# Retention gates between the attention's pairs, decays added to the mask by an accumulating DMA

## The chip, the cores and the metric

The kernel runs on one core of one Trainium2 chip. The metric is the device time of one execution in microseconds (us): the median of three runs was 2032.78 us (2031.46 to 2033.83). A profile was taken of one further execution.

## What is computed

Two transformer blocks for 512 tokens of width 1024, in fp32. The change lies in the second block, which is two layers of this form:

```python
proj = x @ w_in
fq, fk, fv, f_logit, rq, rk, rv, rg = split(proj)
log_f = log_sigmoid(f_logit + b_forget)             # 8 heads
fox_out = fox_attention(fq, fk, fv, log_f)          # softmax(q k / 8 + c_i - c_j), causal, c = cumsum(log_f)
ret = retention(rotary(rq), rotary(rk) / sqrt(128), rv, gamma)   # 4 heads, decays gamma
ret_out = silu(rg) * head_groupnorm(ret)            # rg: the retention gate
x = layernorm(alpha * x + concat(fox_out, ret_out) @ w_out)
x = layernorm(alpha * x + square(relu(x @ w_ff1)) @ w_ff2)
```

The forgetting attention ("fox") has 8 heads of 64, which the kernel works off as four pairs; the retention has 4 heads of 128. The gate `rg` of retention head i is 128 of 512 columns of the projection.

## The kernel before, in words

Every fp32 operand of a matmul is split into a high and a low part (`split2`, line 329: ACT writes the high part, DVE the low one), and a product is three matmuls of 128x512. A weight block is 512 KB: SP loads `wr` (three buffers), ACT makes `wh`, DVE makes `wl` (six buffers each; `wblk`, line 350). `proj_a` (line 414) multiplies one block of 128 columns with all tokens, 24 matmuls into one PSUM bank; `proj_b` (line 419) takes four banks at once, one for each group of 128 tokens, and works through the weights in steps of 24 matmuls.

PSUM has eight banks: four with the tag "mm" for the projections (`mm_ps`, line 301) and four with the tag "at" for the attention and retention (`at_ps`, line 304). A bank is free for the next tile when the last reader of the old one is done.

The order of TensorE's work is written out by a planner, `Weave` (line 160). The main thread issues projections (priority 2); attention pairs and retention heads are threads of priority 1 that cut in when their due time, by the planner's own costs, is reached. A thread yields an event or a number of "at" banks that it needs. TensorE then executes exactly this order. The other engines (ACT, DVE, POOL, and SP, which issues most DMAs) each run their own queue in order; their order is set when the kernel is built, from the order of the code and what is ready.

In a layer of the second block (`block2`, line 1261) the main thread goes through: the values of the attention (line 1263); the forget logits, their cumulative sum, and a DMA that writes it to DRAM as `cd` (line 1270); four times q and k of a pair, after which the pair's thread is spawned (line 1285); the values of the retention (line 1287); four times q and k of a retention head with their rotation, after which its thread is spawned (line 1303); the four gates (line 1304); the output projection (line 1317), whose steps wait for the `mix` tiles they read: 0 to 3 from the attention's pairs, 4 to 7 from the retention heads.

An attention pair (line 507) first splits q and k of each of its two heads out of their PSUM banks (`qs`, `kh`, `kl`), and asks `bias` (line 1194) for the decays: `row` (called `cb` in the code) is a row of `cd` broadcast to 128 partitions by a DMA, and `cm` is that row plus a causal mask `tri`, added by POOL. Scores of a token group then go through DVE (one reduction with `row`, one with `cm` on the diagonal block), ACT (exp), DVE (1/sum) and back to TensorE for transposes and the product with the values.

A retention head (`ret_head`, line 1206) takes the rotated q and k (`ra`: two ACT copies, a DVE and two POOL operations), makes `inner` and the states, normalises on DVE and POOL (`ro`), waits for its gate `sg`, is transposed, multiplied by the gate (`rz`) and split into `mix`. `sg` itself is silu of the gate's projection: three ACT passes and one DVE product (lines 1305 to 1308).

All of these tiles, except weights and small ones, come out of one pool of 56 buffers of 128x512 (`bt`, line 290).

Of the kernel before, what the change touches and what calls it, by code (L numbers as in the profile page):

```python
# [11 lines left out]
F32R = mybir.dt.float32r  # L12
I32 = mybir.dt.int32
AF = mybir.ActivationFunctionType
ALU = mybir.AluOpType
# [4 lines left out]
P, T, D = 128, 512, 1024  # L20
# [13 lines left out]
def _blocks():  # L34

    out = []

    def a(name, l, c0, n, k=D, w=P):
        out.extend((name, l, 0, k, c, c + w, "") for c in range(c0, c0 + n, w))

    def b(name, l, k0, k1, c0):
        out.extend((name, l, k, k + 2 * P, c0, c0 + 512, "") for k in range(k0, k1, 2 * P))

    def low(name, l, c0, n):
        out.append((name, l, 0, D, c0, c0 + n, "low"))

    for c in (0, 512, 1024):
        b("w_in", 0, 0, D, c)
    low("w_in", 0, 3584, 16)
    a("w_in", 0, 1536, 1024)  # L50
    b("w_in", 0, 0, D, 2560)
    b("w_in", 0, 0, D, 3072)
    b("w_in", 0, 0, D, 3600)
    b("w_in", 0, 0, D, 4112)
    for i in range(4):
        for j in range(2):
            a("w_in", 0, 4624 + (2 * i + j) * P, P)
            a("w_in", 0, 5648 + (2 * i + j) * P, P)
        a("w_branch_moba", 0, 256 * i, 256, 512, 256)
        a("w_branch_gla", 0, 256 * i, 256)  # L60
    for n in range(2):
        b("w_out", 0, 0, D, 512 * n)

    def ffn(up, down, l):
        for h in range(2):
            a(up, l, 2048 * h, 2048)
            for n in range(2):
                b(down, l, 2048 * h, 2048 * (h + 1), 512 * n)

    ffn("w_up", "w_down", 0)  # L70
    for l in range(2):
        a("w_in_2", l, 0, 1024)
        low("w_in_2", l, 1536, 8)
        b("w_in_2", l, 0, D, 1024)
        a("w_in_2", l, 1544, 1024)
        b("w_in_2", l, 0, D, 2568)
        a("w_in_2", l, 3080, 512)
        for n in range(2):
            b("w_out_2", l, 0, D, 512 * n)
        ffn("w_ff1_2", "w_ff2_2", l)  # L80
    return out
# [186 lines left out]
def model_kernel(ctx: ExitStack, tc: tile.TileContext, I, out):  # L268
    nc = tc.nc
# [12 lines left out]
    wv = Weave(8 - NM)  # L282
    act, dve, pool = Engine(nc.scalar, wv, 0.2, 0.83), Engine(nc.vector, wv, 0.17, 1.04), Engine(nc.gpsimd, wv, 0.25, 2.1)
    uid = [0]

    def nm(s):
        uid[0] += 1
        return f"{s}_{uid[0]}"

    def bt(s="b", dt=F32):  # L290
        return pb.tile([P, T], dt, tag="b", name=nm(s))

    def at(s="a", dt=F32):
        return pa.tile([P, 4, T], dt, tag="a", name=nm(s))
# [28 lines left out]
    def copy(o, i):  # L323
        act.activation(o, i, AF.Copy)

    def sub_lo(o, x, hi, eng=dve):
        eng.tensor_tensor(o, x, hi.bitcast(F32), ALU.subtract)

    def split2(hi, lo, x, scale=None):

        if scale is None:
            copy(hi, x)
            sub_lo(lo, x, hi)
        else:
            act.activation(hi, x, AF.Copy if isinstance(scale, float) else AF.Identity, scale=scale)
            dve.scalar_tensor_tensor(lo, x, scale, hi.bitcast(F32), ALU.mult, ALU.subtract)
# [35 lines left out]
    class Acts:  # L372


        def __init__(self, n, s, groups=False):
            self.ev = [Event() for _ in range(max(n, NT))]
            if groups:
                self.h = [at(s + "h", F32R) for _ in range(n // 4)]
                self.l = [at(s + "l", F32R) for _ in range(n // 4)]
                self.hs = [self.h[k // 4][:, k % 4, :] for k in range(n)]  # L380
                self.ls = [self.l[k // 4][:, k % 4, :] for k in range(n)]
            else:
                self.hs = [bt(s + "h", F32R) for _ in range(n)]
                self.ls = [bt(s + "l", F32R) for _ in range(n)]

        def split(self, k, x, scale=None):

            split2(self.hs[k], self.ls[k], x, scale)
            wv.mark(self.ev[k])

# [23 lines left out]
    def proj_a(name, l, c, acts, k=8):  # L414
        ps = mm_ps()
        yield from form_a(ps, wblk(name, l, 0, k * P, c, c + P), 0, acts, range(k))
        return ps
# [29 lines left out]
    def const(n):  # L447
        src = const_src(n)
        t = bt(n)[:, 0 : src.shape[1]]
        load(t, src)  # L450
        return t
# [35 lines left out]
    def sigmoid(s, x):  # L487

        act.activation(s, x, AF.Exp, scale=-1.0)
        act.activation(s, s, AF.Ln, bias=one)  # L490
        act.activation(s, s, AF.Exp, scale=-1.0)
# [8 lines left out]
    def row_bcast(src, n0):  # L500

        t = bt("row")
        load(t, bass.AP(tensor=src.tensor, offset=src.offset + n0, ap=[[0, P], [1, T]]))
        return t
# [342 lines left out]
    xw = Acts(8, "xT", True)  # L847
# [342 lines left out]
        yield from block2(0, xw2, h)  # L1190


    def fox_bias(cd, tri):
        def bias(h):
            cb, cm = row_bcast(cd, T * h), bt("cm")
            pool.tensor_tensor(cm, cb, tri, ALU.add)

            def pieces(t):
                d = (P * t, P * t + P, cm[:, P * t : P * t + P])
                return [d] if t == 0 else [(0, P * t, cb[:, 0 : P * t]), d]  # L1200

            return pieces

        return bias
# [56 lines left out]
    def block2(l, xw, h):  # L1261
        fv = []
        yield from proj_b("w_in_2", l, 0, D, 1024, xw, to_tokens(fv, False), tail=8, wait_t=True)
        f = yield from low_proj(wblk("w_in_2", l, 0, D, 1536, 1544, "low"), 8, xw)
        a = bt("fa")
        dve.tensor_scalar(f[0:8], f[0:8], col(f"bf{l}")[0:8], None, ALU.add)
        log_sigmoid(f[0:8], f[0:8], a[0:8])
        dve.tensor_tensor_scan(a[0:8], one[0:8].to_broadcast([8, T]), f[0:8], 0.0, ALU.mult, ALU.add)
        cd = pd.tile([8, T], F32, tag="cd", name=nm("cd"))
        nc.sync.dma_start(cd, a[0:8])  # L1270
        bias = fox_bias(cd, const("tri"))
        mix = Acts(8, "mix")
        for i in range(4):
            qk = []
            for j in range(2):
                qk.append((yield from proj_a("w_in_2", l, 512 * j + P * i, xw)))

            def operands(q, k):
                def get():
                    return q, k, -0.125, None  # L1280
                    yield

                return get

            wv.spawn(attention_pair(i, operands(*qk), fv, bias, mix), 1)
        vs = []
        yield from proj_b("w_in_2", l, 0, D, 2568, xw, to_tokens(vs, False))
        ccos, csin = const("cc"), const("ss")
        decay, xi, zeta = const("decay"), const("xi"), const("zeta")
        sgs = []  # L1290
        for i in range(4):
            qk = []
            for j in range(2):
                ps = yield from proj_a("w_in_2", l, 1544 + 512 * j + P * i, xw)
                a, b = bt("ra"), bt("rb")
                copy(b[0:64], ps[64:128])
                copy(b[64:128], ps[0:64])
                dve.tensor_tensor(a, ps, ccos, ALU.mult)
                pool.tensor_tensor(b, b, csin, ALU.mult)
                pool.tensor_tensor(a, a, b, ALU.add)  # L1300
                qk.append(a)
            sgs.append([Event(), bt("sg")])
            wv.spawn(ret_head(l, i, *qk, vs, decay, xi, zeta, sgs[i], mix), 1)
        for i in range(4):
            ps = yield from proj_a("w_in_2", l, 3080 + P * i, xw)
            ev, sg = sgs[i]
            sigmoid(sg, ps)
            dve.tensor_tensor(sg, ps, sg, ALU.mult)
            wv.mark(ev)
        hT = Acts(8, "hT", True)  # L1310
        ln1 = LayerNorm(h, norm_rows("ln1_g_2", "ln1_b_2", l))

        def norm1(t):
            ln1.apply(t)
            yield from to_features(h[t], hT, t)

        yield from out_proj("w_out_2", l, mix, h, ALPHA, ln1.part, norm1)
        ln2 = LayerNorm(h, norm_rows("ln2_g_2", "ln2_b_2", l))
        if l == 0:
            xw2 = Acts(8, "xT", True)  # L1320

        def norm2(t):
            ln2.apply(t)
            if l == 0:
                yield from to_features(h[t], xw2, t)
            else:
                for n in range(2):
                    nc.sync.dma_start(token_rows(out, t, n), h[t][n])

        yield from ffn("w_ff1_2", "w_ff2_2", l, hT, h, ALPHA, ln2.part, norm2)  # L1330
        if l == 0:
            yield from block2(1, xw2, h)
# [45 lines left out]
```

## Time and profile before

| | |
|---|---|
| median of 3 runs | 2032.78 us |
| profiled execution | 2036.39 us |
| its span | 2034.3 us |
| PE (TensorE matmul) busy | 1992.4 us, 98% |
| DVE busy | 1149.8 us, 57% |
| ACT busy | 954.1 us, 47% |
| POOL busy | 317.7 us, 16% |
| DMA moved | 240.49 MB, 118 GB/s |

The span is the time from the first to the last instruction; the execution's own time is 2.1 us longer. PE's busy share counts matmuls that are pipelined, so it says where PE is idle, not how fast it is.

### The profile page before, as it was taken

The numbers are of one execution on the slowest core, as the hardware profiler recorded it, in microseconds if no ns is written. First come the engines' busy times: TensorE is split into PE (matmuls) and PEld (weight loads), VectorE is DVE, ScalarE is ACT, GpSimd is POOL, SyncE is SP. The second block draws the span as 40 slices with busy tenths as digits, with TensorE's granted clock in tenths as the row PEclk, the third lists the DMA queues.
The fourth block names the chain that finished last, engine by engine and source line by source line (L and its number), as shares of the span: only waits on it lengthen the run. The fifth ranks groups of instructions, "written<-read, shape, count | busy, mean of one in ns | idle before, by whom it ended". The sixth has DMA issues, their size and how long they took to land.

```text
span 2034.3 us, 25413 instructions
## 1 busy us (share of the span) xinstructions
PE 1992.4 (98%) x9478; PEld 1647.8 (81%) x9478; DVE 1149.8 (57%) x2028; ACT 954.1 (47%) x1663; POOL 317.7 (16%) x361
## 2 busy tenths in 40 slices
PE   8999999999999999999999999999999999999997
PEld 6777788888888888877888888888877888888886
DVE  6676444444556573475454656664675554656654
ACT  5666354333545453374333554552564334544551
POOL 2000110000212110011402201112111412211102
PEclk9999999999999999999999999999999999999999
DMA  5422113242766543332232746552422234666541
GB/s 201 156 89 78 52 63 103 94 145 75 185 165 135 155 114 114 103 113 80 73 125 98 165 141 136 144 154 74 140 85 88 68 114 142 138 161 156 133 131 42
DMA packets 93483, 240.49 MB, mean 118 GB/s; under 512 B 10734, under 2 KB 11200, under 8 KB 93360
## 3 DMA queue, kind: packets, MB, share of 16 engines
q1 hardware_dynamic: 72624, 201.12, 29.1%
q0 software_dynamic: 20736, 37.76, 11.5%
q8 instruction: 74, 1.21, 0.2%
q14 instruction: 49, 0.40, 0.1%
HBM read 236.69 MB, written 4.77 MB: 119 GB/s over the span
## 4 chain that ended last, share of the span: by engine, by line
PE 93%; ACT 2%; DVE 1%; POOL 1%; DMA 1%; issue 1%; SPq 0%; POOLq 0%; ACTq 0%; DVEq 0%
PE mm L311 67%; PE at L311 24%; PE at L320 3%; POOL h L262 1%; ACT wh L262 0%; DMA sw<-in_wall_dram 0%; DMA wr<-in_wall_dram 0%; ACT kh L262 0%; ACT qs L262 0%; DVE og L262 0%; DVE qs L262 0%; ACT sil L262 0%; POOL mv L262 0%; ACT h L262 0%; DVE wl L262 0%
## 5 line engine op out<-in xcount | busy, mean ns | idle before, releaser
L262 DVE TENSOR_TENSOR wl<-wr,wh 128x1024 fp32r<-128x1024 f32 (+1 forms) x265 | 337.5, 1275 | 330.6 <-ACT wh L262 329.1
L262 ACT ACTIVATE wh<-wr 128x1024 fp32r<-128x1024 f32 (+1 forms) x268 | 282.6, 1056 | 476.6 <-PE mm L311 328.4
L262 DVE TENSOR_TENSOR wl<-sw,wh 128x512 fp32r<-128x512 f32 x252 | 166.2, 688 | 194.7 <-ACT wh L262 174.2
L262 ACT ACTIVATE wh<-sw 128x512 fp32r<-128x512 f32 x252 | 149.8, 626 | 225.6 <-PE at L311 121.6
L311 PE MATMUL at<-hTh,wh 128*128 128x512 f32 x576 | 224.1, 389 | 0.0
L311 PE MATMUL at<-hTl,wh 128*128 128x512 f32 x576 | 224.1, 389 | 0.0
L311 PE MATMUL at<-hTh,wl 128*128 128x512 f32 x576 | 224.1, 389 | 0.0
L669 POOL DMA_DIRECT2D sw<-in_wall_dram x144 | 127.4, 1056 | 606.3 <-DVE wl L262 481.3
L311 PE MATMUL mm<-xTh,wh 128*128 128x512 f32 x536 | 213.9, 399 | 0.0
L311 PE MATMUL mm<-xTl,wh 128*128 128x512 f32 x536 | 209.0, 390 | 0.0
L311 PE MATMUL mm<-xTh,wl 128*128 128x512 f32 x512 | 199.9, 390 | 0.0
L311 PE MATMUL mm<-wh,xl 128*128 128x512 f32 x504 | 196.2, 389 | 0.7 <-DVE xl L262 0.7
L311 PE MATMUL mm<-wh,xh 128*128 128x512 f32 x504 | 196.2, 389 | 0.1
L311 PE MATMUL mm<-wl,xh 128*128 128x512 f32 x504 | 196.1, 389 | 0.0
L311 PE MATMUL mm<-wh,xTh 128*128 128x512 f32 x352 | 146.6, 416 | 13.1 <-ACT wh L262 6.3
L311 PE MATMUL mm<-wl,xTh 128*128 128x512 f32 x352 | 140.3, 399 | 0.0
L311 PE MATMUL mm<-wh,xTl 128*128 128x512 f32 x352 | 140.0, 398 | 0.0
L311 PEld LDWEIGHTS at<-hTl,wh 128*128 128x128 f32 x576 | 108.1, 188 | 22.6
L311 PEld LDWEIGHTS at<-hTh,wh 128*128 128x128 f32 x576 | 108.1, 188 | 22.4
L311 PEld LDWEIGHTS at<-hTh,wl 128*128 128x128 f32 x576 | 108.1, 188 | 22.3
L311 PEld LDWEIGHTS mm<-xTh,wh 128*128 128x128 f32 x536 | 100.8, 188 | 19.6 <-ACT wh L262 0.5
L311 PEld LDWEIGHTS mm<-xTl,wh 128*128 128x128 f32 x536 | 100.8, 188 | 18.7
(287 smaller groups left out, 3811.1 us busy)
## 6 DMA issues: line engine op xcount, KB each, us to landing
wr<-in_wall_dram SPq DMA_DIRECT2D x266, 512.0 KB, 3.5
sw<-in_wall_dram SPq DMA_DIRECT2D x144, 256.0 KB, 5.7
sw<-in_wall_dram POOLq DMA_DIRECT2D x144, 256.0 KB, 6.0
row<-cd SPq DMA_DIRECT2D x16, 256.0 KB, 4.0
revp<-rev SPq DMA_DIRECT2D x1, 2560.0 KB
xr<-in_xT_dram SPq DMA_DIRECT2D x8, 256.0 KB, 6.1
g<-revp SPq DMA_DIRECT2D x8, 256.0 KB, 4.0
h<-in_x_dram SPq DMA_DIRECT2D x8, 256.0 KB, 5.8
```

What stands on the lines that cost most here:

```text
L262: return f(out, *a, **k)
L311: nc.tensor.matmul(out, lhsT, rhs, start=start, stop=stop, skip_group_check=more)
L320: nc.tensor.transpose(out, in_, ident)
L669: nc.gpsimd.dma_start(t, src, accum_op=ALU.add)
```

## The change

Four edits. The retention gates' projections, with their silu, are moved from behind the retention heads into the loop over the attention's pairs, one behind each pair's q and k. `cm` is no longer made by POOL: for every head the mask `tri` is loaded anew into `cm`'s tile by SP, and a DMA issued by POOL (`nc.gpsimd.dma_start` with `accum_op`) adds the broadcast row of `cd` onto it; `row` is still loaded for the other blocks, and `tri` is no longer kept. The `mix` tiles are taken from the pool when they are first written and not all at once ahead of the pairs. The order of the packed weights in DRAM is that in which the first three groups of a layer are read.

```diff
@@ _blocks
     for l in range(2):
+        b("w_in_2", l, 0, D, 1024)
+        low("w_in_2", l, 1536, 8)
         a("w_in_2", l, 0, 1024)
-        low("w_in_2", l, 1536, 8)
-        b("w_in_2", l, 0, D, 1024)
@@ class Acts
-        def __init__(self, n, s, groups=False):
+        def __init__(self, n, s, groups=False, late=False):
+            self.s = s
...
+            elif late:
+                self.hs, self.ls = [None] * n, [None] * n
...
         def split(self, k, x, scale=None):
+            if self.hs[k] is None:
+                self.hs[k], self.ls[k] = bt(self.s + "h", F32R), bt(self.s + "l", F32R)
@@ fox_bias
-    def fox_bias(cd, tri):
+    def fox_bias(cd):
         def bias(h):
-            cb, cm = row_bcast(cd, T * h), bt("cm")
-            pool.tensor_tensor(cm, cb, tri, ALU.add)
+            cb, cm = row_bcast(cd, T * h), const("tri")
+            nc.gpsimd.dma_start(cm, bass.AP(tensor=cd.tensor, offset=cd.offset + T * h, ap=[[0, P], [1, T]]), accum_op=ALU.add)
@@ block2
-        bias = fox_bias(cd, const("tri"))
-        mix = Acts(8, "mix")
+        bias = fox_bias(cd)
+        mix = Acts(8, "mix", late=True)
+        sgs = []
         for i in range(4):
...
             wv.spawn(attention_pair(i, operands(*qk), fv, bias, mix), 1)
+            ps = yield from proj_a("w_in_2", l, 3080 + P * i, xw)
+            ev, sg = Event(), bt("sg")
+            sgs.append([ev, sg])
+            sigmoid(sg, ps)
+            dve.tensor_tensor(sg, ps, sg, ALU.mult)
+            wv.mark(ev)
...
-        sgs = []
...
-            sgs.append([Event(), bt("sg")])
             wv.spawn(ret_head(l, i, *qk, vs, decay, xi, zeta, sgs[i], mix), 1)
-        for i in range(4):
-            ps = yield from proj_a("w_in_2", l, 3080 + P * i, xw)
-            ev, sg = sgs[i]
-            sigmoid(sg, ps)
-            dve.tensor_tensor(sg, ps, sg, ALU.mult)
-            wv.mark(ev)
```

## Rows read from the trace of the kernel before

**Rows 1.** Table of stretches: start:end, length, busy time of each engine (instructions), clock, DMA.

```profile
780.00:1100.00 320.00, 312.30 (x1571) 257.54 (x1570) 174.59 (x398) 135.84 (x230) 56.80 (x56) 0.99 0.28 93
```

**Rows 2.** The same table inside the attention: PE, PEld, DVE, ACT, POOL, clock, DMA.

```profile
900.00:959.00 59.00, 56.01 (x300) 41.68 (x298) 38.81 (x154) 31.73 (x77) 2.52 (x2) 0.97 0.24 81
...
917.30:920.80 3.50, 3.50 (x12) 2.61 (x11) 1.12 (x2) 0.63 (x1) 2.19 (x2) 0.51 0.00 0
1515.40:1521.40 6.00, 5.93 (x17) 4.76 (x18) 1.83 (x4) 1.47 (x3) 2.50 (x2) 0.50 0.03 12
```

**Rows 3.** Timeline of PE, attention: start, length, instruction, [idle before <-releaser].

```profile
899.52 0.38 PE L311 MATMUL at<-kh,qs 128*128 128x256 f32 x1 [0.86 <-ACT pta L262]
...
909.87 0.39 PE L311 MATMUL mm<-wh,xTh 128*128 128x512 f32 x1
...
916.63 0.50 PE L311 MATMUL mm<-wh,xTh 128*128 128x512 f32 x1 [2.94 <-DVE qs L262]
...
1515.47 0.80 PE L311 MATMUL mm<-wh,xTh 128*128 128x512 f32 x1 [2.95 <-DVE qs L262]
```

**Rows 4.** Timeline of ACT, then DVE, at the splits of pair 3.

```profile
914.62 0.63 ACT L262 ACTIVATE kl<-kl 64x512 fp32r<-64x512 f32 x1 [1.49 <-DVE kl L262]
915.26 0.59 ACT L262 ACTIVATE qs<-mm 64x512 fp32r<-64x512 f32 x1
...
915.88 0.69 DVE L262 SCALAR_TENSOR_TENSOR qs<-mm,qs 64x512 fp32r<-64x512 f32 x1 [1.30 <-ACT qs L262]
```

**Rows 5.** Stretches, matmuls into "mm" banks alone: length, PE busy (matmuls), clock, DMA.

```profile
952.00:1009.00 57.00, 46.55 (x193) 1.00 0.22 74
...
1037.30:1059.20 21.90, 21.71 (x96) 1.00 0.56 181
```

**Rows 6.** Instructions on the tile sg: count, ns min/median/max, first and last start.

```profile
L262 ACT ACTIVATE sg<-mm x8: 577/578/584, 1017.0 to 1638.3; 128x512 f32<-128x512 f32 x8
L262 ACT ACTIVATE sg<-sg,one x8: 722/725/726, 1017.6 to 1638.9; 128x512 f32<-128x512 f32 x8
L262 ACT ACTIVATE sg<-sg x8: 629/632/633, 1018.4 to 1639.7; 128x512 f32<-128x512 f32 x8
L262 DVE TENSOR_TENSOR sg<-mm,sg x8: 691/692/693, 1019.0 to 1640.3; 128x512 f32<-128x512 f32 x8
```

**Rows 7.** Timeline of PE, DVE and POOL at the last retention head.

```profile
1019.45 0.72 PE L311 MATMUL at<-ra,ra 128*128 128x128 f32 x5
...
1041.41 0.60 PE L320 MATMUL at<-ident,ro 128*128 128x128 f32 x4
...
1015.07 0.68 DVE L262 TENSOR_TENSOR ra<-mm,cc 128x512 f32<-128x512 f32 x1
...
1030.03 1.37 DVE L262 TENSOR_SCALAR ro<-at,rm 128x128 f32<-128x128 f32 x4 [1.42 <-POOL rm L262]
...
1043.56 0.69 DVE L262 TENSOR_TENSOR mixl<-rz,mixh 128x512 fp32r<-128x512 f32 x1 [0.76 <-ACT mixh L262]
...
1015.90 1.29 POOL L262 TENSOR_TENSOR ra<-ra,rb 128x512 f32<-128x512 f32 x1 [0.88 <-DVE ra L262]
```

**Rows 8.** The accumulating loads of the FFN (line 669).

```profile
L669 POOL DMA_DIRECT2D sw<-in_wall_dram x144: 862/875/1870, 521.4 to 1934.2; - x144
...
DMA to landing us min/median/max: 3.7/6.0/11.3
```

**Rows 9.** DMA issues: out<-in, queue, count, KB each, median us to landing.

```profile
tri<-in_c_dram SPq DMA_DIRECT2D x2, 256.0 KB, 3.9
```

**Rows 10.** Timeline of SP, POOL and DVE at the first pair.

```profile
863.25 0.38 SPq L348 DMA_DIRECT2D row<-cd  x1
...
867.06 1.29 POOL L262 TENSOR_TENSOR cm<-row,tri 128x512 f32<-128x512 f32 x1 [131.38 <-DMA row<-cd]
...
871.35 2.34 DVE L262 TENSOR_TENSOR wl<-wr,wh 128x1024 fp32r<-128x1024 f32 x1 [0.89 <-ACT wh L262]
...
874.55 0.34 DVE L262 CUSTOM_DVE_ANT_0 ea<-at,cm,mx 128x128 f32<-128x128 f32 x1
```

## The prediction

> **What bounds the kernel now.** I read the busy times first: TensorE (PE) is busy 1992.4 of 2034.3 us, so only its gaps and its slow-clock stretches can be won or lost. Then a table by stage, to see where these lie: the first layer of the second block (780 to 1100 us) has 320.00 - 312.30 = 7.7 us of idle PE [rows 1], and the second layer is alike. Then the same table inside a layer. The forgetting attention (900 to 959 in the first) leaves PE idle for 59.00 - 56.01 = 2.99 us, with a mean clock of 0.97 [rows 2]; the rest of the layer's idle time is at the layer norm behind the output projection, which the change doesn't touch. Last, PE's own instructions in order of time. In both layers one wait is nearly the whole: the third token group of the values' projection (line 1287) stands still 2.94 and 2.95 us until DVE's qs [rows 3]. That is a PSUM bank: the four "mm" banks hold q2, k2, q3, k3 of the last pairs, the values' projection takes four at once, and the third is still being read by pair 3's splits. These stand in ACT's and DVE's queues one behind the other: ACT's kl waits 1.49 us for DVE, the second head's qs is behind it at 915.26, and DVE's qs, which frees the bank, runs at 915.88 [rows 4]. Behind the stall the clock is at 0.51 and 0.50 of full (1.2 instead of 2.4 GHz) for 3.5 and 6.0 us [rows 2], which costs half of that: 1.7 and 3.0 us.
>
> **The change, part by part.** The profiled execution took 2036.39 us; the sum is made against it, and carried over to the median of the runs, 2032.78, which is 3.6 us lower.
>
> *Gates between the pairs.* Four projections a layer move from behind the retention heads to behind each pair. Each brings one weight load, its ACT and DVE splits, 24 matmuls (96 take 21.71 us, so 5.43 [rows 5]), three ACT passes (0.58 + 0.73 + 0.63) and one DVE product (0.69) [rows 6]. None is added or removed, so PE's own work is the same. What moves is cover. Behind k3 there now come 5.43 us of matmuls before the values' projection, plus 2 x 1.36 us of its first two groups, where there were only the 2.7 us. The bank is read until 916.57 (915.88 + 0.69 [rows 4]), 6.7 us after k3's end, where the values' first matmul starts at 909.87 [rows 3]; the second layer is alike; 8.1 us of work cover that. So the stall and its slow clock go: 2.94 + 1.7 + 2.95 + 3.0 = 10.6 us. What is late next is the bank of the last gate itself, held by 1.94 + 0.69 = 2.6 us of ACT and DVE passes, against three groups of 1.36 = 4.1 us; it holds by 1.5 us if neither engine is queued up. The 0.86 us wait for ACT's pta at 899.52 [rows 3] I leave as it is. Bounds for this edit: nothing gained (the wait moves to the gate's bank) to 12.4 (all idle and slow clock of both stages).
>
> *The same move, at the other end.* Before, the 21.7 us of gates lay over the last retention head; now the output projection follows rk3 at once. Let X be the end of rk3, 1009.0: by then the 192 matmuls of the eight retention projections are done (the window shows 193, one being the values' last) [rows 5]. PE has, in its written order behind X: 1.5 us of head 2, three steps of 24 matmuls for mix 0 to 5 (16.3), head 3's own pieces (1.2 + 0.7 + 1.5) and head 2's transposes (0.4): 21.6 us. The fourth step needs mix 7, that is head 3's whole chain. In the recorded order its scores start at 1019.45, X + 10.45; ro, behind the products and their statistics, ends at 1031.40 (1030.03 + 1.37), X + 22.4; then transposes, rz, mixh and mixl, which took from 1041.41 to 1044.25 (1043.56 + 0.69), 2.84 us [rows 7]. Mix 7 is ready at X + 25.2. Of the 3.6 us between, PE can use 0.4 for the transposes, 0.7 for the three matmuls on mix 6, and 0.5 for two that need only mixh: 2.0 us idle. Before that, the output projection's fourth token group takes rk3's bank, which DVE's ra frees at 1015.75 (1015.07 + 0.68, it stands behind head 2's ro), X + 6.75; PE is there at X + 1.5 + 3 x 1.36 = X + 5.6: 1.2 us idle, and head 3's pieces come as much later. Together 3.2 us a layer. Its pieces lie between the wait of 2.94 us, which was followed by slow clock worth 1.7 us, and that of 0.86, which wasn't [rows 2, 3]; with half of 1.7 it makes 4.0 a layer, 8.0 in all. Bounds: 0 (head 3's inputs were there at 1017.2 (1015.90 + 1.29), when POOL's ra had ended, 2.3 us before its matmuls [rows 7], and the written order may put it earlier) to 6 a layer.
>
> *Decays by an accumulating DMA.* Sixteen POOL additions of 1.29 us [rows 10] go; each becomes a load of tri on SP's queue (3.9 us to landing [rows 9]) and a DMA issued by POOL. The nearest row for that one, same size and same form, is the FFN's accumulating load: 0.875 us of POOL, 6.0 us to landing, 3.7 to 11.3 at the ends [rows 8]. POOL has nothing else in this stage. For the first head: row at 863.25, tri behind it 0.4 us later, landed 867.5, accumulated 873.5; cm was ready at 867.06 + 1.29 = 868.35 and first used by DVE at 874.55 [rows 10]. Hidden by 1 us, and less if the plan, which no longer books the addition (1.3 us), starts the scores earlier. Neither tri nor row depends on q or k, so for later pairs they can be issued ahead of the pair. I take 0. Bounds: -1 (DVE's wl took 2.34 us beside POOL's second addition [rows 10]; without one, what is queued behind it on DVE comes up to 1 us earlier) to +10 (next part). The Trainium skill (DMA: Bandwidth & Descriptors, Rules for kernel authors) has it that an accumulating DMA must wait for the semaphore of the load into the same bytes, so that the two landings stand one behind the other; so the code here is written. Its section Anatomy of one DMA gives about 2.0 us plus bytes at 436 GB/s, an estimate of 2.6 us for 256 KB, by which cm would be there at 870.1 and the sum would be the same; the measured 6.0 us decides.
>
> *Late mix tiles and the weights' order in DRAM.* The first gives back up to 16 of 56 buffers during attention, the second changes addresses only; no row shows a wait for a buffer on PE. Cost 0, cover: none needed. The 14 more loads of tri (3.7 MB of 240.5) fall in a layer where the DMA engines are 28% busy [rows 1].
>
> Sum: -10.6 + 8.0 = -2.6 us: 2033.8 for a profiled execution, 2030.2 for the median.
>
> **Rivals.** *The end is covered* (A). If the planner's order and a shorter DVE queue (no gate products there) bring head 3 forward by the 2.3 us it had in hand, the end costs 1 us a layer: -10.6 + 2 = -8.4, 2024.4. For it: the 2.3 us; against: rk3's bank and ro depend on POOL and DVE, not on the order.
>
> *The accumulation lands late* (B), the other side. Place: DVE's first reduction with cm, in each pair. If row and tri are issued only when the pair starts, as in the first pair, cm is there 3.9 + 6.0 = 9.9 us later [rows 8, 9] against 5.1 before (868.35 - 863.25). DVE is in order: behind it wait the pair's exponentials and the next splits of weights, and PE's written order waits at the transposes. It decides from the point where landing comes later than the scores, some 8 us after k's end; at 2 us for three pairs a layer it costs 12 us, less the 2.6: 2042. For it: the first pair has only 1 us in hand. Against: POOL and SP are free, and later pairs had their rows long before use.
>
> *The bank wait only moves* (C): the last gate's passes stand in ACT's queue behind pair 3's splits, the values' projection waits 3 us for that bank with a slow clock after it, and the gate move has bought nothing: -10.6 + 9 + 8.0 = +6.4, 2039. For it: ACT is where the queue stood [rows 4]; against: 1.5 us in hand [rows 6], and pair 3's splits are over by then.
>
> **How the numbers follow.** Forecast 0.45 (2030.2; its own range 2026 to 2035), A 0.25, B 0.18, C 0.12. A measurement of this kernel tells some 0.2% (4.1 us) from no change. Faster by more: A and a quarter of the forecast, 0.36. Slower by more: nearly all of B and half of C, with a small part of the forecast, 0.24. Same 0.40. The range, 2023 to 2041, reaches from just below A to between C and B.
>
> **What would show it.** In PE's timeline there is no idle time in front of the values' third group, and the clock stays at 1.00 through attention; if the wait stands at the fourth group, released by DVE's sg, C is right. Behind rk3 PE waits once for DVE's ra at the fourth group of the output projection and again for mixh or mixl in front of its last step, 2 to 4 us together; none there is A. DVE's reduction with cm starts right behind the one with row; a wait for the accumulating DMA there, and PE waiting at the transposes, is B. The prediction is wrong if the layers' idle time changes in any other place, or if the end costs over 6 us a layer.

## The result, and the profile after

The changed kernel is slower: 2050.76 us (median of 6 runs, 2047.51 to 2054.16) against 2032.47 us (6 runs of the kernel before, 2028.42 to 2034.79), a ratio of 1.0098 with a 95% interval of 1.0087 to 1.0108. The forecast was 2030.2, the range ended at 2041. The profiled execution took 2047.51 us, its span is 2045.7. It is the quickest of the six, which run from a mean granted clock of 0.995 (this one) down to 0.991 (the longest, 2054.16), so part of the median is slow clock that the rows below don't show.

The table of stretches, first layer and its attention, answers to [rows 1] and the first of [rows 2]:

```profile
780.00:1100.00 320.00, 307.72 (x1512) 248.72 (x1511) 167.66 (x395) 134.66 (x228) 54.08 (x56) 0.99 0.33 102
900.00:959.00 59.00, 54.35 (x279) 41.91 (x278) 38.86 (x142) 36.66 (x82) 3.45 (x4) 1.00 0.40 116
```

The attention's clock is at 1.00 (2.4 GHz) now, yet PE's idle time in the layer has grown from 7.7 to 12.3 us. PE's waits over the whole span (engine, line, releaser: total, times, longest) say for what:

```profile
PE at L311 <- DVE mx L262: 9.4, 6, 2.3
...
PE at L320 <- DVE ro L262: 4.8, 8, 0.9
...
PE at L320 <- DVE eb L262: 2.5, 5, 1.2
```

In these two layers the kernel before has none of the three (1.5 us of the 9.4, one wait for `mx`, is in the first block, where the kernel before has 1.6). `mx` is DVE's reduction of the scores, `ro` the normalised retention head, `eb` a block of probabilities to be transposed. The wait of 2.94 us for `qs` [rows 3] has no successor: nothing waits in front of the values' third token group.

How a wait for `mx` comes about, in the timeline of SP, POOL, DVE and PE at the third pair (start, length, instruction, [idle before <-releaser]):

```profile
898.61 14.39 SPq L360 DMA_DIRECT2D wr<-in_wall_dram  x3
913.04 0.42 SPq L348 DMA_DIRECT2D row<-cd  x1
913.56 0.38 SPq L348 DMA_DIRECT2D tri<-in_c_dram  x1
...
919.17 0.86 POOL L1201 DMA_DIRECT2D tri<-cd  x1 [22.87 <-DMA tri<-in_c_dram]
...
920.04 0.55 DVE L262 CUSTOM_DVE_ANT_0 ea<-at,row 128x384 f32<-128x384 f32 x1
...
923.85 0.35 DVE L262 CUSTOM_DVE_ANT_0 ea<-at,tri,mx 128x128 f32<-128x128 f32 x1 [2.91 <-DMA tri<-cd]
...
924.35 0.41 PE L311 MATMUL at<-kh,qs 128*128 128x384 f32 x1 [2.29 <-DVE mx L262]
```

Read it from below. PE waits 2.29 us for a bank that DVE must empty; DVE waits 2.91 us for the accumulating DMA; POOL issued that DMA only when `tri` had landed, 5.6 us after SP asked for it; and SP asked only at 913.56, because three loads of weights stood ahead in its queue and took until 913.0 to go out (the weights have three `wr` buffers). Row and tri asked for, to the first use of the sum: some 10 us, two landings one behind the other. The view of line 1201, which issues the accumulating DMAs, has DVE's waits for them over both layers (us, times) and their landings:

```profile
  DVE ea L262: 17.3, 8
...
DMA to landing us min/median/max: 3.8/4.5/7.1
```

The other new wait, at a retention head (DVE, then PE):

```profile
1006.39 1.37 DVE L262 TENSOR_SCALAR ro<-at,rm 128x128 f32<-128x128 f32 x4 [1.44 <-POOL rm L262]
...
1006.95 1.20 PE L320 MATMUL at<-ident,ro 128*128 128x128 f32 x4 [0.88 <-DVE ro L262]
```

PE comes to the transposes before the first quarter of `ro` is written, waits 0.88 us, and then goes at DVE's pace: four transposes take 1.20 us, where they took 0.60 [rows 7]. All eight heads show it.

### The profile page after: what moved, and what is told of

Read it like the earlier page. It is cut to its first block, busy times and chain, and to the rows that moved or that the text cites. A ratio compares the mean times of both kernels' runs of the same rounds, so it can differ in the third digit from the quotient of the medians.

```text
span 2045.7 us, 25445 instructions
## 1 busy us (share of the span) xinstructions
PE 1996.9 (98%) x9478; PEld 1644.5 (80%) x9478; DVE 1140.5 (56%) x2028; ACT 954.4 (47%) x1663; POOL 309.3 (15%) x361
## 4 chain that ended last, share of the span: by engine, by line
PE 89%; DMA 3%; ACT 3%; DVE 2%; POOL 1%; issue 1%; SPq 0%; POOLq 0%; ACTq 0%; DVEq 0%
PE mm L311 63%; PE at L311 23%; PE at L320 3%; DMA tri<-cd 1%; DMA tri<-in_c_dram 1%; POOL h L262 1%; ACT wh L262 1%; DVE wl L262 1%; ACT kh L262 0%; ACT h L262 0%; POOL rm L262 0%; DVE og L262 0%; DVE rm L262 0%; DVE ea L262 0%; POOL mv L262 0%
```

## The experiments

Each figure below is a median, the ratio (95% interval) is to runs of the kernel before that were measured beside it. "Layers" is a sum read off the timelines: in both layers the time from the first transposes of the layer's input to the first transposes behind its output projection, less the same of the second profile of the kernel before (262.95 and 254.82 us; the experiment `e7_before_again`). It leaves out what the change doesn't touch.

| kernel | us | ratio | layers |
|---|---|---|---|
| changed kernel | 2050.76 | 1.0098 (1.0087 to 1.0108) | +16.8 |
| e1: gates between, POOL adds | 2039.15 | 1.0044 (1.0029 to 1.0059) | +7.8 |
| e2: accumulating DMA, gates as before | 2042.83 | 1.0067 (1.0052 to 1.0082) | +11.0 |
| e3: e1, booked, transposes later | 2036.86 | 1.0031 (1.0019 to 1.0044) | +7.2 |
| e4: changed, transposes later | 2047.30 | 1.0080 (1.0064 to 1.0096) | +15.9 |
| e5: before, one gate between | 2031.51 | 1.0006 (0.9996 to 1.0015) | +0.7 |
| e6: changed, accumulation asked for early | 2046.79 | 1.0072 (1.0055 to 1.0089) | +15.8 |
| e7: before once more | 2032.04 | one run | 0 |
| e8: e6, first tri earlier still | 2035.34 | 1.0025 (1.0015 to 1.0035) | +4.4 |
| e9: e5, last pair's transposes later | 2033.04 | 1.0013 (1.0003 to 1.0023) | +0.6 |
| e10: e1, old mix tiles and DRAM order | 2038.38 | 1.0034 (1.0021 to 1.0047) | +7.6 |
| e11: e8, transposes later | 2031.15 | 0.9994 (0.9985 to 1.0003) | +0.1 |
| e12: two gates between, two at the end | 2032.67 | 1.0005 (0.9996 to 1.0013) | -0.5 |

The last column and the ratios agree within 4 us in each line (1.0098 is 19.9 us), so what follows can be read off the layers, with two things in mind. First, each is one execution, and in four of them the clock falls behind a wait: by estimate (stretches of 2 us at a clock below 0.95, busy time times what is missing to 1) this makes about 5 us of the column in e2 and in e4, 4 in e6 and 2 in e12. In the others, the changed kernel and e7 among them, no such stretch stands in the layers. Second, the changed kernel, e1, e6, e8 and e10 have the same order of PE's instructions in the two layers, so between these only the other engines and the DMAs differ. e7 has that of the kernel before, the rest are ordered in other ways.

**e1: the gate move without the accumulating DMA.**

```diff
-            cb, cm = row_bcast(cd, T * h), const("tri")
-            nc.gpsimd.dma_start(cm, ..., accum_op=ALU.add)
+            cb, cm = row_bcast(cd, T * h), bt("cm")
+            nc.gpsimd.tensor_tensor(cm, cb, tri, ALU.add)
```

> The changed kernel, but the mask plus decays is made by a POOL addition again (outside the planner's bookkeeping, so that its order is drawn up from the same costs), and tri is loaded once a layer: the gate move without the accumulating DMA. Theory (the accumulation lands late in each pair, about 10 us in the profiled execution, and up to 16 if the runs above it wait longer at the same place): 2035 to 2041, with no wait of PE for DVE's mx over 1 us left in the attention, and the four waits for ro in the retention heads still there. Rival 'the moved cover alone costs it' (the end of the layers): 2047 to 2051. Rival 'the accumulation is all of it': 2022 to 2026, the bank stalls being gone.

Measured 2039.15: the accumulation is 0.54% or 11 us of the loss (9.0 by the layers), as the theory has it. But the rest, 9 us (7.8), is there without it: the gate move, which I had down as a gain of 2.6, in the order that the planner writes when the addition isn't booked. No run has the gates moved and the addition booked with nothing else changed. Its waits of PE:

```profile
PE at L320 <- DVE ro L262: 4.8, 8, 0.9
PE at L320 <- DVE eb L262: 3.4, 4, 1.4
```

The waits for `ro` are those of the changed kernel. Of `mx` one wait of 1.6 us is left, the one in the first block. That one landing and an addition are still in time here is close: at the third pair (SP, POOL, DVE)

```profile
912.08 0.90 SPq L348 DMA_DIRECT2D row<-cd  x2
916.79 2.53 POOL L1201 TENSOR_TENSOR cm<-row,tri 128x512 f32<-128x512 f32 x2 [24.75 <-DVE kl L262]
919.85 0.34 DVE L262 CUSTOM_DVE_ANT_0 ea<-at,cm,mx 128x128 f32<-128x128 f32 x1
```

the first sum is ready at 918.1 (half of POOL's 2.53) and used 1.8 us later. In the kernel before, at the same pair,

```profile
893.00 1.28 POOL L262 TENSOR_TENSOR cm<-row,tri 128x512 f32<-128x512 f32 x1 [5.70 <-DMA row<-cd]
908.27 0.33 DVE L262 CUSTOM_DVE_ANT_0 ea<-at,cm,mx 128x128 f32<-128x128 f32 x1
```

it lay ready for 14 us. So with the gates between the pairs the reserve is gone before any accumulating DMA comes in.

Most of e1's loss is not idle time. The stretch of the first layer in e1, then in e7 (length, busy times, clock):

```profile
810.55:1077.43 266.88, 262.70 (x1298) 211.90 (x1297) 142.32 (x362) 118.66 (x208) 49.20 (x46) 1.00 0.28 94
810.02:1072.97 262.95, 259.07 (x1298) 211.73 (x1296) 145.26 (x362) 118.85 (x208) 48.29 (x46) 1.00 0.29 96
```

PE is idle for 4.2 us against 3.9; its busy time is 3.6 us longer, and as much in the second layer. Of these 2.4 a layer are the `ro` transposes at DVE's pace. Another 0.8 are at the first pair's products with the values, 3.2 us from the first to the last where e7 takes 2.4: the second head's wait for ACT's `pta` while those of the first head run, so that PE counts as busy and only its weight loads show the wait:

```profile
890.99 0.13 PEld L311 LDWEIGHTS at<-pta,v 128*64 128x64 f32 x1 [0.62 <-ACT pta L262]
```

**e2: the accumulating DMA with the gates behind the retention heads as before** (the diff is e1's, turned round, on the kernel before).

> The kernel before, with only the accumulating DMA and a tri for each head; the gates stay behind the retention heads. In the kernel before the mask plus decays lay ready 16 to 31 us ahead of its use in the second to fourth pair and 6 to 7.5 us in the first. Theory (the accumulation hurts where the row and tri are issued late against the scores, which the gates between the pairs bring about or at least do not hinder): only the first pair of each layer is late, 2032 to 2038. Rival 'an accumulating DMA is slow wherever it stands': all pairs are late, 2042 to 2050.

Measured 2042.83: the rival's time, and my theory's 2032 to 2038 missed. Not by the rival's mechanism, though: DVE waits for the sum in the first two pairs only. The largest new wait is at the second pair's transposes, once in each layer (ACT, POOL, DVE, PE):

```profile
902.72 0.60 ACT L262 ACTIVATE mixh<-at 128x512 fp32r<-128x512 f32 x1
903.00 0.86 POOL L1196 DMA_DIRECT2D tri<-cd  x1 [12.70 <-DMA row<-cd]
903.36 0.69 DVE L262 TENSOR_TENSOR mixl<-at,mixh 128x512 fp32r<-128x512 f32 x1 [1.32 <-ACT mixh L262]
...
904.10 0.48 PE L320 MATMUL at<-ident,eb 128*128 128x128 f32 x1 [5.40 <-DVE mixl L262]
```

PE waits 5.40 us for a bank, not for the sum: its last reader, `mixl`, stands in ACT's and DVE's queues behind the next pair's splits. Behind the wait the clock is down (length, busy times, clock):

```profile
904.10:909.00 4.90, 4.90 (x14) 4.04 (x15) 4.23 (x23) 2.52 (x8) 0.86 (x1) 0.50 0.67 110
```

The edit does two things at once. POOL's addition is booked in the planner and the DMA is not, so PE's order is another one than in the kernel before: here are the first pair's first scores in e7 and in e2,

```profile
871.65 0.39 PE L311 MATMUL at<-kh,qs 128*128 128x512 f32 x1
869.49 0.39 PE L311 MATMUL at<-kh,qs 128*128 128x512 f32 x1
```

61.6 and 60.3 us behind the layer's first transposes (at 810.02 and 809.22), 1.3 us sooner, as the prediction had said the plan might; farther on, whole blocks have changed places. So e2's 11 us are not the price of the accumulating DMA: about 5 are slow clock, and the order and the late sums are mixed in the rest. The kernel before with an addition that isn't booked would separate them; it wasn't run. That e12 has such a wait for `mixl` where DVE waits for no sum is a hint that the order is enough for it. (The 16 to 31 us of the expectation count from the start of POOL's addition; from its end they are 14 to 30.)

**e3 and e4: the retention heads' transposes due 1.6 us later** in the planner's order, once with POOL's addition, booked again (e3), once in the changed kernel as it is (e4).

```diff
         ev = wv.done()
+        ev.t += 1.6
         yield sg[0]
```

> The changed kernel with POOL's addition again (booked), and each retention head's transposes due 1.6 us later in the planner's order, so that other matmuls stand ahead of them while DVE finishes ro. Theory (both costs are these two): the bank stalls' 10.6 us are won, less some 1 to 2 us a layer at the end: 2022 to 2028, faster than both kernels. Rival 'the end costs what cover it has lost, wherever the transposes stand': the idle time moves to the output projection, 2034 to 2040.

> The changed kernel with the accumulating DMA, and only the transposes of the retention heads due 1.6 us later. Theory: the waits for ro go (2.4 to 4 us a layer), the waits for the accumulating DMA stay: 2042 to 2047. Rival 'the end costs what cover it has lost': 2049 to 2052.

e3, at 2036.86, is in its rival's range and far from the 2022 to 2028 hoped for. The waits for `ro` are gone, and these have come:

```profile
PE at L311 <- ACT pta L262: 2.5, 4, 1.0
...
PE mm L311 <- DVE ra L262: 1.9, 2, 1.0
PE at L311 <- ACT ptc L262: 1.8, 2, 0.9
PE mm L311 <- ACT mixh L262: 1.7, 2, 0.9
```

`ra` and `mixh` stand in the output projection: a bank of rk3 and the last mix tile. These are the two places in which the prediction had looked for the cost of the end. `pta` and `ptc` are in the attention, where the planner has drawn up another order with POOL's addition booked (1.7 us of `pta` stand in the kernel before as well). e4, at 2047.30, just above its theory's range, has the waits for `ra` and `mixh` too, and `mx` as in the changed kernel; the slow clock in its execution hides most of what the transposes give back.

**e5 and e9: one gate between.** If one projection covers the bank, three could stay where they cover the heads. In e9 the last pair's transposes are due 2.2 us later as well.

```diff
             wv.spawn(attention_pair(i, operands(*qk), fv, bias, mix), 1)
...
+        yield from gate(3)
         vs = []
...
-        for i in range(4):
+        for i in range(3):
             ps = yield from proj_a("w_in_2", l, 3080 + P * i, xw)
```

> The kernel before (POOL additions, one tri a layer), with only the last head's gate projection moved: it stands behind the fourth pair, in front of the retention's values, and the other three stay behind the retention heads. Theory (one projection is enough cover for the bank, and three are enough cover for the heads' ro): the waits of 2.94 and 2.95 us go and nothing comes in their place, 2022 to 2026 where the kernel before takes 2029 to 2032. Rival (the wait moves to the gate's bank or to another place in the layer): within 2 us of the kernel before.

> The kernel before with only the last head's gate projection moved in front of the retention's values, and the last pair's transposes due 2.2 us later in the planner's order. Theory (the 2.1 us wait for eb that took the bank wait's place is one of the written order, with other matmuls at hand): it goes, 2024 to 2028, 2 to 5 us faster than the kernel before. Rival (the wait moves on, to the retention heads or to the output projection's last steps): 2029 to 2033.

Neither is faster: e5 is level with the kernel before, as its rival said, e9 0.13% slower. The wait for the bank has gone and two have come, here in e5's waits of PE:

```profile
PE at L320 <- DVE ptb L262: 3.8, 2, 2.0
...
PE mm L311 <- DVE sg L262: 1.7, 2, 0.9
```

and the first of them in its timeline:

```profile
918.70 0.30 PE L320 MATMUL at<-ident,eb 128*128 128x128 f32 x1 [1.96 <-DVE ptb L262]
```

In a layer 2.94 us have become 1.96 + 0.9, the latter in front of the output projection, for the bank of the last gate. The transposes at 918.70 need a bank that DVE's `ptb` frees; in e9 they stood where they had stood (3.7 us in two waits), so they are not the last pair's, and the edit missed its mark.

**e6 and e8: the accumulation asked for early.** e6 makes each pair's row, tri and accumulating DMA ahead of its q and k weights on SP's queue; in e8 the first pair's two tri tiles are also loaded before the decays are computed.

```diff
-            qk = []
+            qk, made = [], [make(2 * i), make(2 * i + 1)]
...
-            wv.spawn(attention_pair(i, operands(*qk), fv, bias, mix), 1)
+            wv.spawn(attention_pair(i, operands(*qk), fv, lambda h, made=made: made[h % 2], mix), 1)
```

> The changed kernel, with row, tri and the accumulating DMA of a pair asked for ahead of the loads of its q and k weights instead of behind them. Theory (it is the late issue on SP's queue that makes DVE wait, and not the accumulation as such): the waits of PE for DVE's mx in the second to fourth pair go, 2038 to 2042, as with POOL's addition (2039.2). Rival (the accumulation itself, its landing beside the weight loads, costs wherever it is issued): 2046 to 2051.

> The changed kernel with row, tri and the accumulating DMA of each pair asked for ahead of its q and k weights, and the first pair's two tri tiles loaded before the decays are computed, so that there the accumulating DMA waits for the decays alone. Theory (an accumulating DMA costs nothing where it has landed before DVE needs it): the 4.3 and 4.5 us in front of the first pair's scores go too, the rest of the layer is as with POOL's additions: 2037 to 2042. Rival (its landing beside the weight loads is late in the first pair whatever is ahead of it): 2044 to 2048.

e6 (2046.79) gave the rival's time, with about 4 us of slow clock in the layers, and its trace shows why. From the second pair on the waits for the sum are gone; in the first it is later than ever (SP, POOL, DVE, PE):

```profile
862.52 0.42 SPq L348 DMA_DIRECT2D tri<-in_c_dram  x1
...
868.59 0.86 POOL L1201 DMA_DIRECT2D tri<-cd  x1 [133.01 <-DVE qs L262]
...
877.67 0.35 DVE L262 CUSTOM_DVE_ANT_0 ea<-at,tri,mx 128x128 f32<-128x128 f32 x1 [2.83 <-DMA tri<-cd]
...
878.17 0.66 PE L311 MATMUL at<-kh,qs 128*128 128x384 f32 x1 [4.12 <-DVE mx L262]
```

Eight rows and tris now go out within 7 us, and from the issue of the accumulating DMA between them to DVE's use are 9.1 us. In e8 (POOL, then DVE at the first pair; SP, POOL and DVE for the second):

```profile
862.84 1.75 POOL L1201 DMA_DIRECT2D tri<-cd  x2 [127.23 <-DVE qs L262]
...
874.02 0.35 DVE L262 CUSTOM_DVE_ANT_0 ea<-at,tri,mx 128x128 f32<-128x128 f32 x1
...
867.22 0.60 SPq L348 DMA_DIRECT2D tri<-in_c_dram  x1
...
873.74 0.86 POOL L1201 DMA_DIRECT2D tri<-cd  x1 [9.15 <-DVE sg L262]
...
895.43 0.35 DVE L262 CUSTOM_DVE_ANT_0 ea<-at,tri,mx 128x128 f32<-128x128 f32 x1
```

The first accumulation goes out at 862.84, 5.7 us sooner, and is used 11 us later; the second pair's lands at about 878 (by the median of 4.5 us for these DMAs in this kernel) and is used at 895. DVE waits for none of them. At 2035.34 e8 is 0.73% (15 us) better than the changed kernel with the same number of accumulating DMAs, and not behind POOL's additions (e1). PE's order is the same in all three, so the cost was when row, tri and sum were asked for; no cost is left to the accumulating DMA as such. e8 also has less of two costs that e1 has: the waits for `eb` (0.5 us instead of 3.4) and the longer products of the first pair (2.4 us instead of 3.2). By the layers the gates, in this order, cost 4.4 us where everything is asked for in time.

**e7: the kernel before once more.**

> The kernel before, unchanged, for a second profile. Theory (the slow clock of 3.5 and 6.0 us behind the bank waits is not in every execution, which is why its median is lower than its profiled execution and why those 4.7 us were never there to be won): the bank waits of 2.9 us stand again at the third token group of the values' projection, and the granted clock behind at least one of them is at 1.00. Rival (the slow clock always follows the wait): 0.5 for some us behind both.

The theory held. PE's wait in the timeline, and the table of stretches behind it in both layers (length, busy times, clock):

```profile
915.27 0.50 PE L311 MATMUL mm<-wh,xTh 128*128 128x512 f32 x1 [2.94 <-DVE qs L262]
```

```profile
917.00:921.00 4.00, 4.00 (x24) 3.33 (x23) 0.89 (x1) 2.41 (x4) 1.19 (x1) 1.00 0.00 0
1513.00:1519.00 6.00, 6.00 (x36) 5.05 (x35) 2.17 (x3) 2.98 (x5) 2.11 (x2) 1.00 0.01 3
```

The same wait of 2.94 us, and behind it 24 matmuls in 4 us at full clock, where [rows 2] had 12 in 3.5 us at 0.51. The span is 2028.6 instead of 2034.3. So the slow clock doesn't follow this wait in every execution.

**e10: mix tiles taken at once and the old order in DRAM,** otherwise e1 (`mix = Acts(8, "mix")`, and the change's first hunk undone).

> The kernel with the gates between the pairs and POOL's additions (2039.2), here with the mix tiles taken at once and the weights in the old order in DRAM. Theory (both are free): 2037 to 2041. Rival (the late tiles or the new addresses have a share in the loss): 2030 to 2036.

2038.38 against 2039.15 for e1, the intervals of the ratios overlap: both edits are free within the noise.

**e11 and e12: what is left to gain.** e11 is e8 with e4's edit; e12 is e8 with only the gates of heads 2 and 3 between, behind the third and fourth pair, and e4's edit for these two heads.

```diff
-            ps = yield from proj_a("w_in_2", l, 3080 + P * i, xw)
...
+            if i > 1:
+                yield from gate(i)
```

> The kernel with all four gates between the pairs and the accumulating DMAs asked for ahead (2035.3), here with the retention heads' transposes due 1.6 us later. Theory (with no gates as cover the end of the layer cannot be had for nothing: the wait for ro turns into one for mix in the output projection): about 3.5 us a layer instead of 5.2, 2030 to 2034, still not faster than the kernel before. Rival (the wait for ro is one of the written order alone): 2022 to 2027.

> As the kernel with the accumulating DMAs asked for ahead, with the gates of heads 2 and 3 behind the third and fourth pair and those of heads 0 and 1 behind the retention heads (heads 2 and 3 with transposes due 1.6 us later). Theory (the gates are cover at both places, and each place needs about two of them): the waits in the attention stay below 2 us a layer and those at the end below 1.5, 2025 to 2029, faster than the kernel before by 2 to 5 us. Rival (what is gained at one place is lost at the other): 2029 to 2033.

e11: 2031.15, as the theory said, no different from the kernel before. Its attention is nearly free of waits; the end isn't (timeline of PE, first layer):

```profile
1032.33 0.50 PE L311 MATMUL mm<-wh,mixh 128*128 128x512 f32 x1 [0.95 <-DVE ra L262]
...
1051.20 0.50 PE L311 MATMUL mm<-wh,mixh 128*128 128x512 f32 x1 [0.86 <-ACT mixh L262]
...
1052.26 0.50 PE L311 MATMUL mm<-wh,mixl 128*128 128x512 f32 x1 [0.33 <-DVE mixl L262]
```

e12: 2032.67, the rival. At the end nothing waits any more; in the attention a wait of the kind seen in e2 is there, 2.2 us at its longest:

```profile
PE at L320 <- DVE mixl L262: 4.3, 2, 2.2
```

The 2 us of slow clock stand behind one of these, so that wait costs more than it lasts.

None of the versions beats the kernel before by more than the interval.

## Why the prediction was wrong, point by point

- **The bank waits go: right. What that is worth, 10.6 us: wrong.** 4.7 of it was slow clock, which e7 shows not to come with the wait every time; I had read a term out of one profiled execution and carried it over to the median. Of the 5.9 us of the waits themselves, e1 gives 3.4 back at the transposes (`eb`), as e5 gives back 1.96 of 2.94. I had named the last gate's bank as what is late next; what was late is the pairs' own chain through DVE. In e8 that wait is down to 0.5 us, so the 5.9 can be had. The rival that moves the wait to the gate's bank did not come about: no wait of PE in the changed kernel is released by `sg`.
- **The end, 4.0 us a layer with bounds of 0 to 6: the place was wrong; that 4.8 came out is luck.** The two waits that I worked out, 1.2 for `ra` and 2.0 for mix 7, are e11's 0.95 and 0.86 + 0.33. In the order that the planner wrote for the changed kernel they never come up, for PE stands earlier at each head's transposes. What I left out: the gate was also what held the transposes back. A head's thread waits for `sg` ahead of them, and in [rows 7] they start at 1041.41, 10 us after `ro` was written. With the gate done early only the planner's estimate of `ro` is left, and it is short by up to 0.9 us; due times 1.6 us later (e3, e4, e11) take these waits away. That costs, a layer, 2.4 us of idle time and 4 x 0.6 us of transposes at DVE's pace: 4.8, or 9.6 over both; rival A's 1 us a layer is out with it. With this, 4.7 us of gain that wasn't owed and the waits for `eb`, the gate move's -2.6 failed as well: by e1 it is +7.8 by the layers, +9 by the ratio.
- **The accumulating DMA, 0: this is the step that failed.** "Neither tri nor row depends on q or k, so for later pairs they can be issued ahead of the pair": they can, but the code asks for them in `bias`, behind the weights of the next projections in SP's queue, and that queue stands still for `wr` buffers (14.39 us). In the kernel before a sum lay ready 14 us ahead of its use at the third pair; with the gates between the pairs 1.8 us are left of that (e1), enough for one landing of 4 us and POOL's 1.3, not for two landings. e1 puts the cost at 11 us (9.0 by the layers), where I had put 0; e8 shows that it is all of lateness. The rival "the accumulation lands late" is what happened: DVE's first reduction with the sum is the place, but PE then waits at the next scores and not at the transposes, and in two or three waits a layer of 0.5 to 2.3 us. That its price of 12 us is near is partly luck. Its time, 2042, was low because it was added to a gate move of -2.6 that is +9.
- **The two landings.** The trace shows the two landings in a chain, 913.56 to 919.17 and on to DVE's use at 923.85. The Trainium skill (DMA: Bandwidth & Descriptors, Rules for kernel authors) asks for just that wait between a load and an accumulation into the same bytes, and advises in the same table to issue a DMA early and to wait for it late; e8 against the changed kernel is that advice worth 15 us. The Trainium skill's 2.0 us plus bytes at 436 GB/s (DMA: Bandwidth & Descriptors, Anatomy of one DMA), by my estimate 2.6 us for 256 KB, is below the shortest landing of the changed kernel's accumulating DMAs, 3.8.
- **Late mix tiles and the order in DRAM, 0: right** (e10).
- **The sum.** Against the undisturbed execution: +11 for the accumulation and +9 for the gates make 20 us by the ratios, 16.8 by the layers; 18.3 was measured between the medians. That the ratios say more than the layers fits the slow clock that the changed kernel's other five runs have and its profiled one hasn't, but only that one has a trace. Of e1's +7.8 the listed waits give +5.4 (9.6 at `ro`, 3.4 at `eb`, less 5.9 for the bank and 1.7 for `pta`, which is in the kernel before at 899.52 [rows 3]); 1.6 more are the first pair's products with the values, and 0.8 I can't put down to one cause. Also open is which order of the queues brings e2's and e12's waits for `mixl`.

## What to carry over

When a load becomes two transfers in series, follow the request back through its issuing queue to the instruction in front of it: what counts is when it can be asked for, and a queue that waits for weight buffers delays everything behind it. Work that is moved away from the end of a stage takes with it the waits that it imposed, and these may be what kept another engine's results out of the way, so ask of each wait that goes what it was holding back. When an edit takes work out of the planner's books, compare the written order before reading its cost. And do not carry a slow-clock stretch of one profiled execution into a median without a second profile.

## What the runs showed of the hardware

- The same wait of PE (2.94 us, same place, same kernel) was followed by a clock of 0.51 (1.2 GHz) for 3.5 us in one execution and by 1.00 (2.4 GHz) in another. Other waits differ likewise: behind e2's 5.40 us the clock was at 0.50 for 4.9 us, behind the changed kernel's 2.29 us it stayed at 1.00.
- The accumulating DMA of 256 KB landed after 4.5 us in the median (3.8 to 7.1) in the changed kernel, below the 6.0 us of the FFN's of the same size [rows 8]; issued amid e6's eight rows and tris of that size, one was 9.1 us from its issue to its use.
- Two heads' products with the values run side by side on PE (in e7 four of 0.62 us within 1.08 us); where one head's operand was late (ACT's `pta`, 0.62 us of waiting in the weight loads), PE showed no idle time and its busy time grew by 0.8 us.
